# Weight splits of the state space part, given precedence over other work of ScalarE and VectorE

## The chip, the cores and the metric

The kernel runs on one core of one Trainium2 chip. The metric is the device time of one execution in microseconds (us). Of three runs of the kernel before, the median is 2339.6 us (2338.9 to 2342.73).

## The reference

Two networks run one after the other on 256 tokens of width 1024, all in float32. The first is one block of grouped-query attention, dilated window attention and a convolutional feed-forward. The second has two layers of a hybrid mixer over the 256 tokens and 256 context tokens: a differential attention beside a state space part (Mamba-2, both directions), merged by gates, and then a squared-ReLU MLP. Only the second network holds the changed part:

```python
xbc = dwconv_silu(xbc_raw, conv_w, conv_b)                # convolution of width 5, then SiLU
xs, bm, cm = jnp.split(xbc, [SSD_D_INNER, SSD_D_INNER + SSD_GROUPS * SSD_STATE], axis=-1)
# ssd_chunked, per direction, chunks of 128 tokens
cs = jnp.cumsum(dt * a, axis=chunk)
chunk_states = einsum(bc, exp(cs[-1] - cs), xc)
h[c + 1] = h[c] * exp(cs[-1]) + chunk_states[c]
y = einsum(cc @ bc.T, exp(cs[l] - cs[s]) below the diagonal, xc) + einsum(cc, h, exp(cs))
# ssd_output
return rmsnorm((yf + yb + d * xs) * jax.nn.silu(z), g) @ w_ssd_o
```

Here xbc_raw, z and the gates are products of the normalised tokens with slices of one wide weight matrix. There are 8 groups of 4 heads of 64, with a state of 128.

## The kernel before, in words

Activations lie transposed: 128 channels on the partitions, tokens along the free dimension. A float32 product is made of three float32r matmuls: weights and activations are both split in a high half, rounded to float32r, and a low half, the rest. `wload` (line 129) fetches 1 MB of weights (1024 rows, 256 columns) by a DMA on SP's queue into one of three `raw` buffers, and `wsplit` (line 138) makes of it two 128-column pieces, each with a copy to `whi` on ScalarE (line 145) and a subtraction to `wlo` on VectorE (line 146). Pool `whl` has four buffers of each half (line 820), that is two loads. A piece is then used by 24 matmuls (line 356), which take `hhi*whi`, `hlo*whi` and `hhi*wlo` in turn for eight steps of 128 rows.

`ssd` (line 1427) runs the state space part of a layer, with 512 tokens in layer 0 and 256 in layer 1 (the context's states are needed there too). It goes through 8 groups. For each group `front_g` makes B, C and x (tiles psB, psC, psxs, and after the convolution `conv` on VectorE the tiles BT, CT and xT) one group ahead, `z_g` makes the gate z (psz), and `fill_g` puts in products of other parts by a plan: in layer 0, groups 0 to 3 carry an attention output block with its gate (psga, psao), groups 4 to 6 carry none, group 7 a gate (psgs); in layer 1 most groups carry one block. In group 7, `so_g` begins the output product (psso).

The group's own work stands between these products. B and x are turned (ptB, ptx); `wx` scales x (tile xw, line 1553, VectorE) and `state` multiplies it with B into psst; `advance` makes the next state (hst, lines 1569 to 1572). `decay` builds the decay matrices E (lines 1590 to 1598) and R (1600, 1602) on ScalarE and VectorE from a row that a DMA on SP's queue spreads (`R<-csd`); `output` multiplies them with x and the states into psy. `decay` for the third and fourth chunk is traced right after the first and second `output`.

The order on TensorE is written out: with `self.pin` every matmul is kept in the order in which it is traced, and `Stream` feeds the products in steps between the group's own work. On ScalarE, VectorE and SP the framework's planner orders the queues when the program is built: among the instructions that it takes as ready at a moment it issues the one that was traced first. `high_priority(offset=n)` makes instructions count as if they had been traced n instructions earlier; the attention part uses it with 250 (`SOON`). On the chip each of these queues then runs in the planned order.

Of the kernel before, what the change touches and what calls it, by code (L numbers as in the profile page):

```python
# [12 lines left out]
F32 = mybir.dt.float32  # L13
# [12 lines left out]
ADD, SUB, MUL, MIN, MAX = ALU.add, ALU.subtract, ALU.mult, ALU.min, ALU.max  # L26
# [40 lines left out]

SOON = 250

CUTS = [slice(a, b) for a, b in ((0, 2), (2, 4), (4, 6), (6, 8))]  # L70

NWARM = 12
# [41 lines left out]
class Build:  # L114
    def __init__(self, tc, aps, es, stop=None):
        self.tc, self.nc, self.a, self.es, self.stop = tc, tc.nc, aps, es, stop
        self.pin = False

    def pool(self, name, bufs=1, space=None, reuse=None, side=None):
        kw = {} if side is None else {"side": side}  # L120
        if space is not None:
            kw["space"] = space
        if reuse:
            kw["reuse_waits"] = reuse
        return self.tc.tile_pool(name=name, bufs=bufs, **kw)
# [10 lines left out]
    def wsplit(self, raw, nk, cols):  # L136
        nc = self.nc
        w = []
        for c in range(0, cols, 128):
            n = min(128, cols - c)  # L140
            hi = self.whl.tile([P, 8, 128], F32R, tag="whi", name="whi")
            lo = self.whl.tile([P, 8, 128], F32R, tag="wlo", name="wlo")
            r = raw[:, :nk, c:c + n]
            h = hi[:, :nk, :n]
            nc.scalar.copy(h, r)  # L145
            nc.vector.tensor_tensor(out=lo[:, :nk, :n], in0=r, in1=h.bitcast(F32), op=SUB)  # L146
            w.append((hi, lo))
        return w

    def wloadB(self, src, pool, bufs):  # L150

        nc = self.nc
        raw = self.wraw.tile([P, 8, 256], F32, tag="raw", name="raw")
        nc.sync.dma_start(raw, src)
        hi = pool.tile([P, 8, 256], F32R, tag="whB", name="whB", bufs=bufs)
        lo = pool.tile([P, 8, 256], F32R, tag="wlB", name="wlB", bufs=bufs)
        for ks in (slice(0, 4), slice(4, 8)):
            self.split(hi[:, ks], lo[:, ks], raw[:, ks])
        return hi, lo
# [76 lines left out]
    def rsqrt(self, v, pool, n, tag="nw"):  # L236
        nc = self.nc
        p = v.shape[0]
        ti = pool.tile([p, n], F32, tag=tag + "t", name="nwt")
        y = pool.tile([p, n], F32, tag=tag + "y", name="nwy")  # L240
        nc.vector.tensor_scalar(out=ti.bitcast(I32), in0=v.bitcast(I32), scalar1=1, scalar2=None,
                                op0=ALU.arith_shift_right)
        nc.vector.tensor_scalar(out=y.bitcast(I32), in0=ti.bitcast(I32), scalar1=-1.0,
                                scalar2=float(0x5F3759DF), op0=MUL, op1=ADD)
        for _ in range(3):
            nc.vector.tensor_tensor(out=ti, in0=y, in1=y, op=MUL)
            nc.vector.scalar_tensor_tensor(out=ti, in0=ti, scalar=-0.5, in1=v, op0=MUL, op1=MUL)
            nc.vector.scalar_tensor_tensor(out=y, in0=ti, scalar=1.5, in1=y, op0=ADD, op1=MUL)
        return y

    def fnorm(self, src, kts, n, dim, pool):

        nc = self.nc
        acc = pool.tile([P, n], F32, tag="sqa", name="sqa")
        for i, k in enumerate(kts):
            if i == 0:
                nc.scalar.activation(out=acc, in_=src(k), func=AF.Square)
            else:
                sq = pool.tile([P, n], F32, tag="sq", name="sq", bufs=2)
                nc.scalar.activation(out=sq, in_=src(k), func=AF.Square)  # L260
                nc.vector.tensor_tensor(out=acc, in0=acc, in1=sq, op=ADD)
        return self.rstd([acc], n, dim, pool, root=False)
# [202 lines left out]
    def block1(self, xl, xc):  # L465
# [4 lines left out]
        with ExitStack() as es:  # L470
# [9 lines left out]
            wkv = [wf.tile([P, 8, 256], F32R, tag=n, name=n, bufs=2) for n in ("whB", "wlB")]  # L480
            for ks in CUTS:
                nc.sync.dma_start(xl[:, ks, :], a["x"][:, ks, :])
# [9 lines left out]
            with self.tc.manual_schedule(engines={ENG.DVE, ENG.Activation}):  # L492
                for ks in CUTS:
                    for k in range(ks.start, ks.stop):
# [932 lines left out]
    def ssd(self, l, hx, NQ, att):  # L1427
        nc, a = self.nc, self.a
        lat_only = NQ == 256
        tq = slice(0, NQ)  # L1430
        self.yd = None if lat_only else self.dr.tile([8, P, 512], F32, tag="yd", name="yd")
        ys = []
        SQ = self.ssq = self.cp.tile([P, 512], F32, tag="ssq", name="ssq")
        with ExitStack() as es:
            wk = es.enter_context(self.pool("ssd", reuse="tile"))
# [71 lines left out]
            for g in range(8):  # L1507
# [164 lines left out]
                for y, u in zip(yt, us):  # L1672
                    nc.vector.scalar_tensor_tensor(out=y, in0=y, scalar=0.5, in1=u, op0=MUL, op1=MUL)
                    if g == 0 and y is yt[0]:
                        nc.gpsimd.tensor_tensor(out=SQ, in0=y, in1=y, op=MUL)
                    else:
                        nc.scalar.activation(out=u, in_=y, func=AF.Square)
                        (nc.gpsimd if g < 7 else nc.vector).tensor_tensor(out=SQ, in0=SQ, in1=u, op=ADD)
                for j in range(2):
                    kt = 2 * g + j  # L1680
                    y = yy[j]
                    if self.yd is not None and kt < 8:
                        nc.sync.dma_start(self.yd[kt], y)
                        ys.append(None)
                    else:
                        if not lat_only or j == 0:
                            yhi = self.op.tile([P, 512], F32R, tag="op", name="yhi")
                            ylo = self.op.tile([P, 512], F32R, tag="op", name="ylo")
                        o = slice(j * 256, j * 256 + 256) if lat_only else slice(0, 512)
                        self.ysplit(l, kt, yhi[:, o], ylo[:, o], y)  # L1690
                        ys.append((yhi[:, o], ylo[:, o]))
        return ys

    def so_g(self, l, ys, NQ, c, i, ps=None):
# [448 lines left out]
```

## Time and profile before

| | us |
|---|---|
| median of 3 runs | 2339.6 |
| profiled execution | 2343.83 |
| its span, first to last instruction | 2342.0 |
| TensorE busy | 2297.6 |
| VectorE busy | 1821.4 |
| ScalarE busy | 1349.2 |

The granted TensorE clock is 0.998 of full speed over the span. The state space part of layer 0 lies at about 600 to 1066 us of the span, that of layer 1 at about 1757 to 2085 us. Busy times are of the engine, without its queue's waits. A matmul's end is modelled, so TensorE's busy share says little of how near it is to its peak; its idle time is what its queue waited for. In a list of waits a row reads: who waited, for whom, us in total, times, longest. In a timeline a row reads: start, duration, engine, line, operation, output and inputs, count, and in brackets the engine's idle time before it with what ended it.

### The profile page before, as it was taken

How to read it: one execution, taken by the hardware profiler on the slowest of the kernel's cores; microseconds unless marked ns; L12 is line 12 of the kernel's file. 1: busy time of each engine (PE TensorE's matmuls, PEld its weight loads, DVE VectorE, ACT ScalarE, POOL GpSimd, SP SyncE). 2: the span in 40 equal slices, each digit the busy share in tenths (PEclk: the TensorE clock that was granted, in tenths of full speed). 3: DMA queues.
4: the chain of work that ended last, by engine and by line, in shares of the span. 5: the costliest groups of instructions: out<-in, count | busy, mean ns of one | idle time of the engine just before them, and what ended most of it. 6: DMA issues, size and time to landing. Idle time of an engine off the chain costs nothing.

```text
span 2342.0 us, 38252 instructions
## 1 busy us (share of the span) xinstructions
PE 2297.6 (98%) x14840; PEld 2001.8 (85%) x14840; DVE 1821.4 (78%) x3601; ACT 1349.2 (58%) x2692; POOL 51.0 (2%) x61
## 2 busy tenths in 40 slices
PE   8999999999999999999999999999999999999998
PEld 8889989888887787778897878799898888899997
DVE  7678867877787788996476667488788999977887
ACT  5666546777666567774243223247776767655553
POOL 0000000000000000000000000000000000000000
PEclk9999999999999999999999999999999999999999
DMA  7557574212433334336235555362234535265553
GB/s 287 206 187 255 203 262 146 75 55 73 126 126 119 126 115 143 97 130 234 99 126 194 201 205 206 110 218 97 74 113 127 179 132 167 99 222 184 186 180 109
DMA packets 75894, 362.81 MB, mean 155 GB/s; under 512 B 9280, under 2 KB 16448, under 8 KB 38464
## 3 DMA queue, kind: packets, MB, share of 16 engines
q1 hardware_dynamic: 71952, 355.61, 44.4%
q10 hardware_dynamic: 3760, 4.75, 0.6%
q8 instruction: 117, 1.92, 0.3%
q14 instruction: 65, 0.53, 0.1%
HBM read 346.44 MB, written 13.89 MB: 154 GB/s over the span
## 4 chain that ended last, share of the span: by engine, by line
PE 73%; DVE 13%; ACT 9%; DMA 3%; issue 2%; SPq 0%; DVEq 0%; ACTq 0%
PE psm L356 20%; PE psxs L356 7%; PE psso L356 6%; PE psu L356 5%; PE psz L356 5%; PE psga L356 3%; PE pso L356 2%; PE psao L356 2%; PE psd L356 2%; PE psB L356 2%; PE psy L356 2%; DVE wlo L146 2%; PE psgs L356 2%; DMA araw<-in_ada 2%; PE psC L356 2%
## 5 line engine op out<-in xcount | busy, mean ns | idle before, releaser
L145 ACT CAST whi<-raw 128x1024 fp32r<-128x1024 f32 (+1 forms) x430 | 445.6, 1043 | 501.9 <-PE psm L356 234.2
L146 DVE TENSOR_TENSOR wlo<-raw,whi 128x1024 fp32r<-128x1024 f32 (+1 forms) x430 | 522.3, 1219 | 113.5 <-ACT whi L145 110.9
L356 PE MATMUL psm<-hhi,whi 128*128 128x258 f32 (+2 forms) x544 | 179.1, 329 | 1.7 <-ACT whi L145 1.2
L356 PE MATMUL psm<-hlo,whi 128*128 128x258 f32 (+2 forms) x544 | 178.5, 328 | 0.4 <-DVE hlo L1017 0.3
L356 PE MATMUL psm<-hhi,wlo 128*128 128x258 f32 (+2 forms) x544 | 178.1, 327 | 0.5 <-DVE wlo L146 0.5
L1590 ACT ACTIVATE E<-R,cstok 128x128 f32<-128x128 f32 x384 | 119.8, 391 | 37.8 <-PE psy L356 29.0
L356 PEld LDWEIGHTS psm<-hhi,whi 128*128 128x128 f32 x544 | 103.3, 190 | 16.0 <-ACT whi L145 4.3
L356 PE MATMUL psxs<-hhi,whi 128*128 128x512 f32 x256 | 112.6, 440 | 0.0
L356 PEld LDWEIGHTS psm<-hlo,whi 128*128 128x128 f32 x544 | 103.3, 190 | 10.6 <-DVE hlo L1017 1.2
L356 PE MATMUL psm<-dh,whi 128*128 128x512 f32 (+1 forms) x320 | 111.1, 347 | 0.5 <-DVE x L1902 0.5
L356 PEld LDWEIGHTS psm<-hhi,wlo 128*128 128x128 f32 x544 | 103.4, 190 | 9.4 <-DVE wlo L146 0.7
L356 PE MATMUL psm<-dl,whi 128*128 128x512 f32 (+1 forms) x320 | 111.1, 347 | 0.0
L356 PE MATMUL psm<-dh,wlo 128*128 128x512 f32 (+1 forms) x320 | 111.1, 347 | 0.0
L356 PE MATMUL psxs<-hhi,wlo 128*128 128x512 f32 x256 | 100.3, 392 | 0.0
L356 PE MATMUL psxs<-hlo,whi 128*128 128x512 f32 x256 | 100.2, 391 | 0.0
L1263 ACT ACTIVATE pr<-pss,mx 128x512 f32<-128x512 f32 (+1 forms) x96 | 58.4, 615 | 65.6 <-DVE mx L1261 65.3
L1450 DVE SCALAR_TENSOR_TENSOR xT<-psxs,halfw,xT 128x508 f32<-128x508 f32 (+1 forms) x128 | 94.9, 744 | 0.3
L356 PE MATMUL psu<-hhi,whi 128*128 128x256 f32 x320 | 91.4, 286 | 0.5 <-ACT hhi L897 0.5
L356 PE MATMUL psu<-hlo,whi 128*128 128x256 f32 x320 | 90.6, 283 | 0.8 <-DVE hlo L898 0.8
L356 PE MATMUL psz<-hhi,whi 128*128 128x512 f32 (+1 forms) x256 | 91.3, 356 | 0.0
L356 PE MATMUL psu<-hhi,wlo 128*128 128x256 f32 x320 | 90.5, 283 | 0.0
L356 PE MATMUL psm<-dhl,whi 128*128 128x512 f32 x256 | 89.5, 393 | 0.0
(500 smaller groups left out, 7105.6 us busy)
## 6 DMA issues: line engine op xcount, KB each, us to landing
raw<-in_w_m SPq DMA_DIRECT2D x68, 1024.0 KB, 4.9
araw<-in_ada SPq DMA_DIRECT2D x54, 1024.0 KB, 5.1
R<-csd SPq DMA_DIRECT2D x48, 512.0 KB, 6.0
raw<-in_w_up SPq DMA_DIRECT2D x22, 1024.0 KB, 5.0
raw<-in_w_qk SPq DMA_DIRECT2D x16, 1024.0 KB, 4.9
raw<-in_w_bc SPq DMA_DIRECT2D x16, 1024.0 KB, 5.2
raw<-in_w_xs SPq DMA_DIRECT2D x16, 1024.0 KB, 4.9
raw<-in_w_z SPq DMA_DIRECT2D x16, 1024.0 KB, 5.0
```

The lines of the kernel that those rows point to most:

```text
L145: nc.scalar.copy(h, r)
L146: nc.vector.tensor_tensor(out=lo[:, :nk, :n], in0=r, in1=h.bitcast(F32), op=SUB)
L356: i = self.nc.tensor.matmul(*args, **kw)
L1263: nc.scalar.activation(out=pt_[:, i * kw:(i + 1) * kw], in_=ps[:, i * kw:(i + 1) * kw], func=AF.Exp, scale=0.125, bias=mx[:, i:i + 1], acc ...
L1450: nc.vector.scalar_tensor_tensor(out=y[:, :, lo:hi], in0=u[:, :, lo + o:hi + o], scalar=wj(j), in1=y[:, :, lo:hi], op0=MUL, op1=ADD)
L1590: nc.scalar.activation(out=E[:, d, h, :], in_=R[:, d, h, :], func=AF.Relu, scale=-1.0, bias=self.cs_tok[:, c, i:i + 1])
```

## The change

A constant 150 is added. While `ssd` runs, `wsplit` issues its copy and its subtraction under `high_priority` with that offset. The tiles are allocated and the DMA is issued outside of it. Outside of `ssd` the offset is zero and nothing is different.

```diff
+WSOON = 150
...
         self.pin = False
+
+        self.wsoon = 0
...
             r = raw[:, :nk, c:c + n]
             h = hi[:, :nk, :n]
-            nc.scalar.copy(h, r)
-            nc.vector.tensor_tensor(out=lo[:, :nk, :n], in0=r, in1=h.bitcast(F32), op=SUB)
+            with self.tc.high_priority(offset=self.wsoon) if self.wsoon else ExitStack():
+                nc.scalar.copy(h, r)
+                nc.vector.tensor_tensor(out=lo[:, :nk, :n], in0=r, in1=h.bitcast(F32), op=SUB)
             w.append((hi, lo))
...
         ys = []
+        self.wsoon = WSOON
         SQ = self.ssq = self.cp.tile([P, 512], F32, tag="ssq", name="ssq")
...
                         ys.append((yhi[:, o], ylo[:, o]))
+        self.wsoon = 0
         return ys
```

## Rows read from the trace of the kernel before

**Rows 1.** The page, busy time: us, share of the span, instructions.

```profile
PE 2297.6 (98%) x14840; PEld 2001.8 (85%) x14840; DVE 1821.4 (78%) x3601; ACT 1349.2 (58%) x2692; POOL 51.0 (2%) x61
```

**Rows 2.** Busy time by stretch: stretch, length, busy us (instructions) by engine, clock, DMA.

```profile
690.00:886.00 196.00, 196.00 (x1040) 157.41 (x1040) 155.08 (x267) 121.46 (x260) 8.59 (x6) 1.00 0.41 130
918.00:1051.00 133.00, 129.91 (x740) 100.10 (x740) 127.93 (x237) 102.16 (x235) 9.46 (x6) 1.00 0.36 116
1783.00:1821.00 38.00, 36.19 (x205) 30.52 (x206) 36.58 (x63) 25.08 (x44) 0.00 (x0) 1.00 0.25 84
1821.00:2054.00 233.00, 232.90 (x1612) 203.66 (x1610) 220.14 (x357) 164.57 (x324) 8.89 (x6) 1.00 0.44 146
```

**Rows 3.** Waits of TensorE in the state space part of layer 0.

```profile
PE psst L356 <- DVE hst L1572: 1.5, 3, 0.8
PE psz L356 <- DVE wlo L146: 1.5, 2, 0.9
PE psy L356 <- DVE E L1598: 1.3, 2, 1.1
...
PE psB L356 <- DVE wlo L146: 0.2, 1, 0.2
```

**Rows 4.** Waits of TensorE in the state space part of layer 1.

```profile
PE psz L356 <- DVE wlo L146: 1.3, 1, 1.3
...
PE ptx L351 <- DVE xT L1454: 0.5, 1, 0.5
```

**Rows 5.** Timeline, layer 0, group 6: the second half of z.

```profile
993.60 1.05 ACT L145 CAST whi<-raw 128x1024 fp32r<-128x1024 f32 x1
...
1014.65 1.21 DVE L146 TENSOR_TENSOR wlo<-raw,whi 128x1024 fp32r<-128x1024 f32 x1
...
1015.92 0.50 PE L356 MATMUL psz<-hhi,wlo 128*128 128x512 f32 x1 [0.91 <-DVE wlo L146]
```

**Rows 6.** VectorE's groups of instructions, 918 to 1051: count, busy us, mean ns.

```profile
L146 DVE TENSOR_TENSOR wlo<-raw,whi 128x1024 fp32r<-128x1024 f32 x18 | 22.6, 1258 | 0.0
```

**Rows 7.** Timeline, layer 0, end of group 6: VectorE and TensorE.

```profile
1010.51 0.44 PE L356 MATMUL psy<-E,xd 128*64 128x128 f32 x4
...
1021.96 0.68 DVE L1598 TENSOR_TENSOR E<-E 128x512 f32<-128x512 f32 x1
...
1022.82 1.21 DVE L146 TENSOR_TENSOR wlo<-raw,whi 128x1024 fp32r<-128x1024 f32 x1
...
1022.82 0.44 PE L356 MATMUL psy<-E,xd 128*64 128x128 f32 x4
...
1024.28 0.50 PE L356 MATMUL psz<-hhi,whi 128*128 128x512 f32 x1
```

**Rows 8.** Timeline, layer 1: groups 0 and 2, around the first xw and psst.

```profile
1803.65 1.29 DVE L1553 TENSOR_TENSOR xw<-xd,dk 128x512 f32<-128x512 f32 x2
...
1805.47 1.02 PE L356 MATMUL psst<-xw,Bt 128*128 128x512 f32 x2
...
1878.15 1.04 ACT L145 CAST whi<-raw 128x1024 fp32r<-128x1024 f32 x1
...
1879.92 0.69 DVE L1553 TENSOR_TENSOR xw<-xd,dk 128x512 f32<-128x512 f32 x1
...
1880.03 1.04 ACT L145 CAST whi<-raw 128x1024 fp32r<-128x1024 f32 x1
...
1882.66 0.59 PE L356 MATMUL psst<-xw,Bt 128*128 128x512 f32 x1
...
1885.85 1.22 DVE L146 TENSOR_TENSOR wlo<-raw,whi 128x1024 fp32r<-128x1024 f32 x1
```

**Rows 9.** Waits of ScalarE and VectorE, 690 to 886, groups 1 to 3 of layer 0.

```profile
ACT whi L145 <- PE psz L356: 21.4, 6, 4.0
...
DVE wlo L146 <- ACT whi L145: 10.8, 10, 3.5
```

## The prediction

> **What bounds the kernel now.** I read the page first, then busy time by stretch, then who waits for whom on TensorE in the two state space parts, and last the order of single instructions around those waits.
>
> The page shows TensorE (PE) busy 98% of the span and VectorE (DVE) 78% [rows 1]. A busy PE need not be at its peak, but no order on other engines shortens a matmul; what this change can win lies in PE's idle time inside the state space parts. By stretch [rows 2] there are two regimes. In the plain groups PE never rests: 196.00 of 196 us in groups 1 to 3 of layer 0 and 232.90 of 233 in groups 1 to 6 of layer 1. In groups 4 to 7 of layer 0, which carry less filler for PE, and in the first group of layer 1, DVE is nearly full (127.93 of 133, 36.58 of 38) and PE is short: 133 - 129.91 = 3.1 and 38 - 36.19 = 1.8 us. PE's idle time in the four stretches is 0 + 3.1 + 1.8 + 0.1 = 5.0 us. The waits name the causes: in layer 0 psz and psB wait 1.5 + 0.2 us for a low half (wlo), psst 1.5 for hst, psy 1.3 for E [rows 3]; in layer 1 psz waits 1.3 for wlo, ptx 0.5 for xT [rows 4].
>
> **The change, part by part.** No instruction is added or removed, and the load's DMA on SP's queue keeps its place in the trace; only the 128-wide copies on ScalarE (ACT) and subtractions on DVE may go forward in their queues. They go past what was traced up to 150 instructions before them. In the full stretch of layer 0, 740 + 237 + 235 + 6 instructions take 133 us, 9.2 a us; in layer 1, 1612 + 357 + 324 + 6 take 233 us, 9.9 a us [rows 2]. So 150 stand for some 15 to 16 us (an estimate: it takes the planner's count as the profile's).
>
> *What goes.* The late low halves are late by their place in DVE's queue, not by their data: the second half of z in group 6 has its high half from 993.60, and DVE takes up the low half only at 1014.65; PE idles 0.91 us for it [rows 5]. With 15 us of precedence this one starts well before its use. All waits for low halves go: 1.5 + 0.2 + 1.3 = 3.0 us.
>
> *What is late next.* A low half takes 22.6 / 18 = 1.26 us in the full stretch [rows 6]. DVE has 133 - 127.93 = 5.1 us of idle time there [rows 2], so 1.26 us put in front of something is 1.26 us taken from it unless a gap takes it up. The next in line is E for the last psy of a group: it ends at 1021.96 + 0.68 = 1022.64, psy starts at 1022.82, and the low half for the next block begins only then [rows 7]. This E is traced after the psy two before its own, at 1010.51; the next load, group 7's z, is traced at its use, 1024.28 [rows 7]. The 13.8 us between them are less than 16, so both its halves can go ahead of E: 2 x 1.26 - 0.18 = 2.3 us of new wait. The bounds are 0 (the gaps of 5.1 us swallow it) and 2.3; I take 2.3, since that row shows DVE in step with PE and no gap before E. It is paid once and not in each group: in a stretch where DVE sets the pace, PE's total delay is fixed by the worst single point, and later waits shrink by what the earlier one took.
>
> In the first group of layer 1 the first xw ends about half way through the pair that begins at 1803.65 and takes 1.29, near 1804.3; psst uses it at 1805.47 [rows 8], a margin of about 1.1. Two low halves of 1.22 ahead of it cost 2.4 - 1.1 = 1.3 us. Bounds: 0 (they find a gap) and 1.3; I take 1.3, because this stretch has 38 - 36.58 = 1.4 us of DVE idle in all.
>
> In the plain groups of layer 1 (six in the stretch) the first xw ends at 1879.92 + 0.69 = 1880.6 and psst starts at 1882.66: 2.0 us of margin. The first high half of z starts at 1878.15 and is done at 1879.2, ahead of xw; the second starts at 1880.03, behind it [rows 8]. One low half ahead costs 1.22 < 2.0, so nothing; two would cost 0.4 in each of six groups, 2.6 us. I take 0 and keep 2.6 for the range. In groups 1 to 3 of layer 0 DVE has 196 - 155.08 = 41 us of idle time [rows 2] as cover, and most splits cannot move anyway (third rival): 0.
>
> *ACT and the buffers.* There are four buffers of each half, so a copy can start only when PE has done with the half four back. A copy that is first in ACT's queue holds everything behind it meanwhile: in groups 1 to 3 of layer 0 ACT stood 21.4 us in 6 such waits for psz, at most 4.0 us each, and DVE then 10.8 us in 10 waits for the copy [rows 9]. Earlier copies lengthen these waits. I take 0, since ACT has 233 - 164.57 = 68 us and DVE 13 us to spare in the plain groups of layer 1; without that cover it is the second rival. The Trainium skill says the same of the engines (TensorE: Matmul & The Clock Gate, "Architectural detail: the array is 16x 32x32, not 1x 128x128"): ScalarE and VectorE work their queues strictly first in, first out. The trace agrees with it in those 4.0 us, and it speaks against putting a waiting instruction forward.
>
> The Trainium skill's Perfetto Trace Analysis, "Optimization Strategy", advises to take the gaps of the bounding engine and to make what ends them start sooner. By that alone only the 3.0 us count and the time would be 2339.6 - 3.0 = 2336.6; here the engine that ends the gaps is itself full, which the 1.26 us above stand for.
>
> **Sum.** -3.0 + 2.3 + 1.3 + 0 = +0.6 us. The profiled execution took 2343.8 (span 2342.0 and 1.8 around it), which gives 2344.4; the runs' median of 2339.6 lies 4.2 lower, and I forecast by it: 2339.6 + 0.6 = 2340.2 us. What this kernel's measurement can tell from no change is about 0.2%, 4.7 us.
>
> **Rivals.**
> 1. *Faster: DVE's gaps take the early halves.* If the 5.1 us of DVE idle in layer 0 absorb what moves forward, and the raw buffers, free sooner, let loads start sooner, all of PE's 5.0 us may go: 2334.6. For it: the low halves are the largest single cause of waits. Against: the other 2.0 us have other causes (hst, E, xT), which early splits delay. Chance of more than 0.2%: 0.13.
> 2. *Slower: the queues stand at the split.* Place: z's and the fillers' copies in the six plain groups of layer 1. DVE idles 233 - 220.14 = 12.9 us there, 2.1 a group; from the point where the new standing exceeds 2.1 us a group, PE waits for all above. One standing of 4.0 us [rows 9] in every group costs 1.9 x 6 = 11 us; with the +0.6 and the 2.6 of xw that is 2354, and in half of the groups 2347. For it: 94% DVE, four buffers. Against: ACT has much slack, and copies already stand first there. Chance of more than 0.2%: 0.24.
> 3. *It changes little.* Where a copy already starts as its buffer comes free and the low half follows at once, as in the waits of [rows 9], precedence has nothing to overtake; only the full stretches change order, and a full DVE gives back what it gets. Time 2339.6. This shares the 0.63 of "within 0.2%" with my forecast.
>
> **How the numbers follow.** Likeliest is the forecast with the third rival: 0.63 within 0.2% (about 0.40 and 0.23). Faster 0.13, slower 0.24, as the first and second rival. The lower end is the first rival rounded, 2334: more than PE's 5.0 us can hardly go. The upper end is the second in somewhat over half the groups, 2349. Its own range for the likeliest case is 2336.6 (the 3.0 us go and nothing comes) to 2343 (+0.6 and 2.6).
>
> **What would show it right or wrong.** Right: PE's waits for wlo gone in both parts; low halves begin within a few us of their high halves in groups 5 to 7 of layer 0; there the waits of psst and psy for hst, xw and E grow by 1 to 3 us; the plain groups keep PE without idle time, as now. Wrong on the fast side: PE idle in layer 0's full stretch under 1.5 us with E still in time. Wrong on the slow side: PE waits of 1 us and more in the plain groups of layer 1, with longer waits of ACT for psz or psxs ahead of them; or DVE's idle time there above 13 us. If the low halves of group 6 still lag 20 us, the precedence does not reach as far as I take it to.

## The result: 18 us slower, and the profile after

The changed kernel took 2359.05 us in the median of 6 runs (2354.27 to 2363.47), the kernel before beside it 2340.96 in 6 runs (2338.9 to 2342.73): a ratio of 1.0079, 95% interval 1.0068 to 1.0089, or 18.1 us. The forecast was +0.6 us. The profiled execution took 2360.97 us, with a span of 2359.2 us against 2342.0, 17.2 us more. Matched matmul by matmul with the trace of before, it is 0.9 us late where layer 0's state space part begins and 6.8 where that ends, 5.4 where layer 1's begins and 17.2 where that ends: 5.9 us are lost in the one part and 11.8 in the other.

The work is the same. The page's first part has the same instructions, and VectorE's busy time, 1820.4 us, is that of [rows 1] within 2 us:

```profile
PE 2304.6 (98%) x14840; PEld 2008.0 (85%) x14840; DVE 1820.4 (77%) x3601; ACT 1351.1 (57%) x2692; POOL 50.4 (2%) x61
```

Busy time by stretch, the same four stretches of work as in [rows 2], moved by the delay so far. A row has the stretch, its length, the busy time of PE, PEld, DVE, ACT and POOL, the granted clock, and the DMA's share and rate:

```profile
691.00:888.00 197.00, 196.96 (x1047) 158.00 (x1047) 155.70 (x267) 122.62 (x263) 8.69 (x6) 1.00 0.40 130
919.00:1058.00 139.00, 131.19 (x742) 102.17 (x740) 128.26 (x236) 101.61 (x234) 8.85 (x6) 0.98 0.36 113
1790.00:1828.00 38.00, 35.84 (x197) 30.09 (x197) 35.24 (x60) 22.95 (x42) 0.00 (x0) 0.96 0.32 103
1828.00:2073.00 245.00, 237.81 (x1626) 207.16 (x1624) 220.41 (x359) 167.38 (x326) 8.70 (x6) 0.99 0.43 139
```

Groups 1 to 3 of layer 0 still run without idle time. The three others do not: PE idles 139 - 131.19 = 7.8 us where it idled 3.1, 38 - 35.84 = 2.2 where it idled 1.8, and in the six plain groups of layer 1 245 - 237.81 = 7.2 where it idled 0.1. That is 12.2 us more. VectorE idles more too (245 - 220.41 = 24.6 us in the plain groups, 12.9 before): it does not have more to do, it does it in a worse order. The clock of these three stretches is below 1.00 as well.

What PE waits for, in layer 0 and then in layer 1; the columns are the engine, the operation and what ended its wait, then us in total, times and the longest. They answer to [rows 3] and [rows 4]:

```profile
PE psst L361 <- DVE xw L1559: 6.6, 2, 3.7
PE psy L361 <- DVE E L1604: 1.8, 3, 1.1
PE psst L361 <- DVE hst L1578: 0.8, 1, 0.8
```

```profile
PE psy L361 <- DVE hst L1578: 5.6, 3, 2.1
PE ptx L356 <- DVE xT L1460: 2.2, 1, 2.2
PE psst L361 <- DVE xw L1559: 1.5, 1, 1.5
```

No wait for a low half is left in the two parts: the change did what it says, and its 3.0 us went. In groups 4 to 7 of layer 0 a low half now starts 0.7 us after its high half is done in the median and 4.4 at most, where it was 12.0 and 22.9. In their place stand waits for the state chain (xw, hst) and for xT, each long and in one piece. The two of 6.6 us stood at 954.01 (2.92 us, group 5) and 1002.38 (3.71 us, group 6). VectorE's queue around the second, in order of time (start, duration, instruction):

```profile
992.87 0.68 DVE L1559 TENSOR_TENSOR xw<-xd,dk 128x512 f32<-128x512 f32 x1
...
994.12 1.21 DVE L151 TENSOR_TENSOR wlo<-raw,whi 128x1024 fp32r<-128x1024 f32 x1
...
997.06 1.22 DVE L151 TENSOR_TENSOR wlo<-raw,whi 128x1024 fp32r<-128x1024 f32 x1
998.20 0.74 DVE L1456 SCALAR_TENSOR_TENSOR CT<-psC,halfw,CT 128x508 f32<-128x508 f32 x1
...
1001.16 0.74 DVE L1456 SCALAR_TENSOR_TENSOR CT<-psC,halfw,CT 128x508 f32<-128x508 f32 x1
1001.82 0.75 DVE L1559 TENSOR_TENSOR xw<-xd,dk 128x256 f32<-128x256 f32 x2
```

Two low halves, four steps of C's convolution, four steps of hst and two of E now stand between the second and the third xw (the row of 1001.82 holds the third and the fourth), and PE stands from 998.67 to 1002.38 for that third xw. In the kernel before, one low half, one step of C and one of hst stood between the same two:

```profile
990.51 0.67 DVE L1553 TENSOR_TENSOR xw<-xd,dk 128x512 f32<-128x512 f32 x1
...
991.76 1.21 DVE L146 TENSOR_TENSOR wlo<-raw,whi 128x1024 fp32r<-128x1024 f32 x1
...
994.49 0.41 DVE L1553 TENSOR_TENSOR xw<-xd,dk 128x256 f32<-128x256 f32 x1
```

From one xw to the other it is 8.95 us where it was 3.98. Of these 5.0 us the added low half takes 1.1; the three added steps of C take 2.0, those of hst 1.0 and of E 0.9. So the precedence did not only put pieces of 1.2 us in front of a fixed order: the planner set the order anew, and xw came out behind the convolution. In layer 1 the same happens to hst. Of group 2, first VectorE and then PE:

```profile
1888.31 1.21 DVE L151 TENSOR_TENSOR wlo<-raw,whi 128x1024 fp32r<-128x1024 f32 x1
...
1893.08 1.21 DVE L151 TENSOR_TENSOR wlo<-raw,whi 128x1024 fp32r<-128x1024 f32 x1
...
1899.95 1.23 DVE L151 TENSOR_TENSOR wlo<-raw,whi 128x1024 fp32r<-128x1024 f32 x1
...
1903.27 1.21 DVE L151 TENSOR_TENSOR wlo<-raw,whi 128x1024 fp32r<-128x1024 f32 x1
...
1906.06 1.21 DVE L151 TENSOR_TENSOR wlo<-raw,whi 128x1024 fp32r<-128x1024 f32 x1
1907.19 0.68 DVE L1460 SCALAR_TENSOR_TENSOR xT<-cth,xT 128x512 f32<-128x512 f32 x1
1907.79 0.41 DVE L1578 TENSOR_TENSOR hst<-hst,psst 128x256 f32<-128x256 f32 x1
```

```profile
1908.26 0.44 PE L361 MATMUL psy<-R,hst 128*64 128x128 f32 x4 [2.06 <-DVE hst L1578]
```

Five low halves, and behind the last of them the hst that PE waits 2.06 us for. Low halves are not denser than before; more of them stand ahead of this hst. Before, three stood between the first xw of the group (1879.92, [rows 8]) and this step, at 1885.85, 1887.64 and 1892.08, and it came 14.6 us after that xw:

```profile
1892.08 1.23 DVE L146 TENSOR_TENSOR wlo<-raw,whi 128x1024 fp32r<-128x1024 f32 x1
...
1894.47 0.42 DVE L1572 TENSOR_TENSOR hst<-hst,psst 128x256 f32<-128x256 f32 x1
```

Now it comes 20.7 us after it (1887.05 to 1907.79). Of the 6.2 us more, the two added low halves take 2.3, added steps of x's convolution 2.6. Groups 4 and 6 have the like at 1988.95 (1.95 us) and 2065.74 (1.60), group 5 a wait for xw at 2011.77 (1.48).

There is a second cost. The granted clock, by stretches of a few us:

```profile
951.00:954.00 3.00, 0.09 (x1) 0.02 (x1) 3.00 (x7) 0.67 (x2) 0.00 (x0) 1.00 0.86 319
954.00:957.00 3.00, 2.99 (x14) 2.54 (x14) 3.00 (x8) 1.15 (x4) 0.00 (x0) 1.00 0.02 8
...
1001.00:1007.00 6.00, 4.62 (x11) 3.70 (x12) 5.85 (x15) 2.43 (x6) 0.00 (x0) 0.50 0.24 101
...
1803.00:1806.00 3.00, 0.84 (x8) 0.61 (x7) 2.48 (x4) 2.03 (x3) 0.00 (x0) 1.00 0.00 0
1806.00:1810.00 4.00, 4.00 (x15) 3.08 (x14) 3.76 (x7) 1.22 (x2) 0.00 (x0) 0.57 0.42 119
1906.00:1909.00 3.00, 0.94 (x14) 0.74 (x12) 2.80 (x5) 0.63 (x1) 0.00 (x0) 0.94 0.35 55
1909.00:1912.00 3.00, 3.00 (x20) 2.67 (x17) 0.45 (x1) 2.44 (x8) 0.00 (x0) 0.50 0.87 347
```

From 1000.7 for 6.8 us, from 1806.3, 1908.7 and 1990.6 for 3.4 us each, the clock was at its lower level (0.50, which is 1.2 of 2.4 GHz); each began during a stall of 1.95 us or more or within 1.7 us of its end. The stall of 2.92 us that ended at 954.01 was followed by none. The kernel before has no such stretch in these parts. (A fifth, from 464.8, lies ahead of all that was changed; this execution loses 1.6 us there.) PE was busy for 5.12 + 3 x 3.4 = 15.3 us of them, and at half the clock up to 15.3 / 2 = 7.7 us of that is lost. With the 12.2 us of idle time it makes 19.9, an upper bound for the 17.2 us by which the span grew.

One stall shows the price of a stretch. In layer 1's first group PE waits 2.16 or 2.17 us for xT in six profiles. In three of them (the changed kernel, act_only, chain_after) 3.4 us at the lower clock go with it, and from the matmul at 1783 to the one at 1821 they lose 1.7, 1.7 and 1.7 us against the kernel before; in the others (dve_only, l1_only, pool_after) there are none, and they lose 0.2 each. So 3.4 us at the lower clock cost some 1.5 us there, and the 17 us of such stretches in the two parts some 7.5, an estimate.

### The profile page after: what moved, and what is told of

It reads as the page before. It is cut to its first block, busy times and chain, and to the rows that moved or that the text cites. A ratio compares the mean times of both kernels' runs of the same rounds, so it can differ in the third digit from the quotient of the medians.

```text
span 2359.2 us, 38322 instructions
## 1 busy us (share of the span) xinstructions
PE 2304.6 (98%) x14840; PEld 2008.0 (85%) x14840; DVE 1820.4 (77%) x3601; ACT 1351.1 (57%) x2692; POOL 50.4 (2%) x61
## 4 chain that ended last, share of the span: by engine, by line
PE 73%; DVE 14%; ACT 8%; DMA 3%; issue 2%; SPq 0%; DVEq 0%; ACTq 0%
PE psm L361 18%; PE psxs L361 6%; PE psso L361 6%; PE psu L361 5%; PE psz L361 5%; PE psao L361 3%; PE psga L361 3%; DVE wlo L151 3%; PE pso L361 2%; PE psd L361 2%; PE psy L361 2%; PE psB L361 2%; DMA araw<-in_ada 2%; PE psgs L361 2%; PE psC L361 2%
```

## Experiments

Each time is a median, beside runs of the kernel before on the same chip: 2340.87 us for the first four, 2341.55 for the next four, 2342.71 for the last four.

| run | us | ratio, 95% interval | us more |
|---|---|---|---|
| act_only | 2344.60 | 1.0016 [1.0007, 1.0025] | 3.7 |
| dve_only | 2361.14 | 1.0081 [1.0064, 1.0097] | 20.3 |
| l0_only | 2348.29 | 1.0032 [1.0020, 1.0044] | 7.4 |
| l1_only | 2348.42 | 1.0034 [1.0020, 1.0047] | 7.6 |
| chain_after | 2343.66 | 1.0013 [1.0003, 1.0022] | 2.1 |
| chain_before | 2347.81 | 1.0028 [1.0016, 1.0040] | 6.3 |
| off50 | 2343.62 | 1.0009 [0.9999, 1.0019] | 2.1 |
| z_only | 2347.03 | 1.0023 [1.0013, 1.0032] | 5.5 |
| pool_before | 2354.62 | 1.0050 [1.0037, 1.0063] | 11.9 |
| pool_after | 2356.87 | 1.0066 [1.0054, 1.0078] | 14.2 |
| l1_best | 2339.94 | 0.9989 [0.9980, 0.9997] | -2.8 |
| best | 2350.66 | 1.0041 [1.0029, 1.0053] | 8.0 |

**Which engine's queue.** The theory was VectorE's order; the rival, the prediction's second, that ScalarE's queue stands at copies whose buffer is not free. Each half of the change alone:

```diff
 # act_only: the copy alone has the precedence
+            with self.tc.high_priority(offset=self.wsoon) if self.wsoon else ExitStack():
+                nc.scalar.copy(h, r)
             nc.vector.tensor_tensor(out=lo[:, :nk, :n], in0=r, in1=h.bitcast(F32), op=SUB)
 # dve_only: the subtraction alone has it
             nc.scalar.copy(h, r)
+            with self.tc.high_priority(offset=self.wsoon) if self.wsoon else ExitStack():
+                nc.vector.tensor_tensor(out=lo[:, :nk, :n], in0=r, in1=h.bitcast(F32), op=SUB)
```

> Only the copies on ScalarE keep the precedence; the subtractions on VectorE go by their trace place again. Theory A (VectorE's order: low halves taken ahead of xw, hst and xT make TensorE wait): most of the loss goes, 2340 to 2346 us, TensorE's waits for xw and hst in the two state space parts under 3 us together. Theory B (ScalarE's queue stands at copies whose buffer is not free and holds back what VectorE needs): the loss stays, 2352 to 2360 us.

> Only the subtractions on VectorE keep the precedence. Theory A: the loss stays, 2352 to 2360 us, with waits of TensorE for xw and hst of 8 us and more. Theory B: 2339 to 2345 us, with ScalarE's waits for buffers as in the kernel before.

The subtraction alone costs all of it, 20.3 us, just above the range expected. The two stalls of psst in layer 0 are there, 3.10 and 3.70 us. PE's waits of dve_only in layer 1:

```profile
PE psst L361 <- DVE xw L1559: 5.5, 5, 1.5
PE ptx L356 <- DVE xT L1460: 2.2, 1, 2.2
PE psst L361 <- DVE hst L1578: 1.5, 2, 1.2
PE psy L361 <- DVE hst L1578: 1.1, 1, 1.1
```

In act_only, ScalarE does stand longer in the plain groups of layer 1, as the rival says (its waits there for psxs to free a buffer are 18.9 us, where before has 12.0), yet from the second group on PE's longest wait is 0.7 us; the xT of the first row is that of the first group:

```profile
ACT whi L150 <- PE psxs L361: 18.9, 8, 4.7
```

```profile
PE ptx L356 <- DVE xT L1460: 2.2, 1, 2.2
PE ptx L356 <- ACT xd L1550: 1.1, 2, 0.7
```

The rival is refuted as the main cause. One stall is its work all the same, that of xT in layer 1's first group. Of the changed kernel, ScalarE and then VectorE:

```profile
1803.20 1.04 ACT L150 CAST whi<-raw 128x1024 fp32r<-128x1024 f32 x1 [1.66 <-PE psC L361]
1804.15 0.62 ACT L1459 ACTIVATE cth<-xT 128x512 f32<-128x512 f32 x1
...
1804.81 0.69 DVE L1460 SCALAR_TENSOR_TENSOR xT<-cth,xT 128x512 f32<-128x512 f32 x1 [0.52 <-ACT cth L1459]
```

A copy stands 1.66 us for its buffer with the tanh of x's convolution (cth) behind it, and VectorE idles for that tanh before it makes the xT that PE waits 2.16 us for. In the kernel before this tanh ran at 1796.84, ahead of the copy at 1797.76. The same copy waits the same 1.66 us ahead of xT in act_only, dve_only and chain_after. The 3.7 us of act_only come with this late xT and 3.4 us at the lower clock behind it, and with waits for E and hst in layer 0 of 1.1 us at most.

**Which layer.**

```diff
 # l0_only
+        self.wsoon = 0 if lat_only else WSOON
 # l1_only
+        self.wsoon = WSOON if lat_only else 0
```

> Precedence in layer 0 alone. By the trace of the change, where layer 0's part came out 5.5 us later: 2346 us (2343 to 2349), with the two waits of psst for xw, 2.9 and 3.7 us, as in the full change, and nothing different in layer 1. If the two layers act on each other, it differs by more than 3 us.

> Precedence in layer 1 alone. By the trace of the change, 11 to 12 us later there, of which some 4 us stretches at half the clock: 2352 us (2347 to 2355). If the clock falls less often, near 2348.

By the medians the layers share the loss about equally (intervals of 4.7 to 10.3 and 4.7 to 11.0 us), and each shows the stalls that it has in the full change: 2.91 and 3.70 us for xw in l0_only, 2.16 for xT, 1.83, 1.94 and 1.60 for hst and 1.48 for xw in l1_only. The sum, 15.0 us, is 3.1 short of 18.1, which lies within the two intervals. The runs of l1_only differ with the clock: at a mean of 0.999 they took 2346.78 and 2346.99 us, at 0.998 2348.42 and 2348.55, and the profiled one at 0.996 2354.18. Not all of these 7 us is the layer's: of the profile's five stretches at the lower level two, of 3.4 us each, lie in its part. The one run of the full change at 0.998 took 2354.27, 13.3 us above the median of before.

**Is it the state chain?** If the loss comes from xw and hst behind low halves, putting these ahead again must take most of it away; put ahead without the change, they show what they cost by themselves.

```diff
 # chain_after: on the changed kernel; chain_before: the same on the kernel before
+                    with self.tc.high_priority(offset=300):
                         (the product xw)
+                        with self.tc.high_priority(offset=300):
                             (the two steps of hst in `advance`)
```

> The full change, and xw and the two steps of hst (VectorE) get precedence over the splits (offset 300). Theory A (the loss is the place of xw and hst behind low halves in VectorE's queue): TensorE's waits for xw and hst go from 14 us to under 3, the clock falls less, 2339 to 2345 us. Rival C (VectorE is simply full, and what is put first only decides what is late next): 2350 us and more, with new waits for E, xT or the convolution's tiles.

> The kernel before with the same precedence for xw and hst alone. Theory A: the waits of psst for hst and xw, 1.5 us in layer 0, go and little else changes: 2338 to 2341 us. Rival C: those of E and of the low halves grow by as much, 2341 to 2345 us.

chain_after gives back 16 of the 18 us. In layer 1 of its profile the waits of psy for hst and of psst for xw are gone, and of the group's own work only the xT of the first group is late, beside 0.3 us of psst for hst; in layer 0 the waits for xw are gone, and E, the next in line, is late instead:

```profile
PE psy L361 <- DVE E L1606: 6.6, 4, 3.0
...
PE ptx L356 <- DVE xT L1460: 2.2, 1, 2.2
```

chain_before is slower than either theory expected, and shows the other side of a full VectorE. There the state chain comes early and z's low half is late, once by 7.87 us, with 10.2 us at the lower clock. Its wait, then the instruction:

```profile
PE psz L356 <- DVE wlo L146: 9.0, 2, 7.9
```

```profile
1014.92 0.80 PE L356 MATMUL psz<-hhi,wlo 128*128 128x512 f32 x1 [7.87 <-DVE wlo L146]
```

**A smaller dose.**

```diff
 # off50
+WSOON = 50
 # z_only: WSOON = 150, set around z's loads in the groups alone
```

> The change with an offset of 50, about 5 us of the trace. Theory A: a split passes only what was traced less than a third as far back, so xw and hst, traced 2 to 4 us before their use, are still passed but by fewer splits: 2341 to 2348 us. If the loss does not depend on how far the splits come forward, 2355 us and more.

> Precedence for the loads of z alone, the only ones besides one of psB for which TensorE waited in the kernel before. Theory A: psz's waits (2.8 us) go, xw and hst still stand behind z's low halves in layer 1's groups and in groups 5 and 6 of layer 0: 2344 to 2354 us. If precedence hurts through other loads (x, B, C), 2338 to 2342 us.

A third of the reach costs 2.1 us, an interval that holds no change: PE waits 4.2 us for hst and 3.8 for E in layer 0, none longer than 1.7, and the clock stays up in both parts. z's loads alone bring back one stall of 4.0 us in layer 0, a stretch of 6.8 us at the lower clock that begins in it, and 5.5 us. Neither wins anything in all.

**Is VectorE's load or its order the limit in layer 0?** GpSimd is nearly idle there, so z's low halves of groups 4 to 7 went to it.

```diff
 # pool_before: on the kernel before; pool_after: on the changed one
+            (nc.gpsimd if self.lo_pool else nc.vector).tensor_tensor(out=lo[:, :nk, :n], ...
+                self.lo_pool = l == 0 and g > 3     # around z's loads
```

> The kernel before, with one edit: the low halves of z's weight in groups 4 to 7 of layer 0 (8 of them) are subtracted by GpSimd, which is idle there, instead of VectorE. Theory A (VectorE is full in that stretch, so whatever stands last in its queue makes TensorE wait, and order alone cannot win): 8 x 1.26 = 10 us leave VectorE, its idle time there rises from 5 to some 15 us, TensorE's waits in layer 0 fall from 5.2 to under 3 us, 2337 to 2340. Rival (the order of VectorE's queue alone makes the waits, its load does not): TensorE's waits stay at 4 to 5 us, 2341 within 1. Should GpSimd's subtraction take so long, or slow VectorE's own work so much, that the halves come late, TensorE waits for the low half for several us a group: 2345 and more.

> The full change, with the low halves of z's weight in groups 4 to 7 of layer 0 on GpSimd. Theory A: the two single stalls of psst in layer 0 (2.9 and 3.7 us) shrink to under 1 us each and the slow-clock stretch behind the second goes, while layer 1 keeps its own loss of some 7 us: 2347 to 2351. Rival (the stalls come from order, of which load takes no part, for example from the fillers' low halves ahead of xw): the two stalls stay above 2 us, 2355 to 2360.

Both miss the range of their theory. The expectation of pool_before allowed for a slowed VectorE, but through low halves that come late, and none is late. GpSimd's subtractions and, below them, what VectorE did in the same moments in pool_before:

```profile
996.53 2.38 POOL L147 TENSOR_TENSOR wlo<-raw,whi 128x1024 fp32r<-128x1024 f32 x1 [5.47 <-ACT whi L146]
1005.94 2.40 POOL L147 TENSOR_TENSOR wlo<-raw,whi 128x1024 fp32r<-128x1024 f32 x1 [7.03 <-ACT whi L146]
1011.01 2.37 POOL L147 TENSOR_TENSOR wlo<-raw,whi 128x1024 fp32r<-128x1024 f32 x1 [2.67 <-ACT whi L146]
```

```profile
996.83 2.62 DVE L1556 TENSOR_TENSOR xw<-xd,dk 128x512 f32<-128x512 f32 x1
...
1006.17 2.45 DVE L1649 TENSOR_TENSOR hst<-hst,dec 128x256 f32<-128x256 f32 x1
...
1009.87 0.41 DVE L1574 TENSOR_TENSOR hst<-hst,dec 128x256 f32<-128x256 f32 x1
...
1011.13 2.92 DVE L1600 SCALAR_TENSOR_TENSOR E<-cb,dttok,E 128x128 f32<-128x128 f32 x3
```

An xw of 0.68 us takes 2.62, a step of hst of 0.41 takes 2.45, and each ends 0.3 to 0.7 us after GpSimd's instruction does. What reads PSUM was not held: the BT step on psB at 947.11, beside the subtraction from 946.50 to 949.43, took its 0.73 us. Nor was an xw that began with that subtraction, at 946.51 (0.68 us). All six subtractions between 918 and 1062 us show it; the excess of the six VectorE entries that they hit is 1.94 + 2.04 + 2.05 + 1.5 + 2.0 + 1.6 = 11.1 us (the groups of E against three times 0.29 and against 1.13). What left VectorE is 6 x 1.26 = 7.6. So by these entries the move loads VectorE by 3.5 us where it is fullest, in lumps of 2 us (over the whole stretch, 921 to 1064.3, it is busy 133.1 us where it was 127.9), and 11.9 us are lost. In pool_after the stalls of 2.9 and 3.7 us for xw are gone and the longest waits of psst are 1.84 and 1.83 us, for hst; but psy waits 1.82 for E, and layer 1 has its own loss; the time is the rival's, the shorter stalls are the theory's. Whether load is the limit in layer 0 can't be told from this, since the load did not fall.

**A better order for layer 1.** There VectorE has some 2 us to spare in each group. l1_best leaves layer 0 as it was and orders layer 1 by what PE needs first; best adds the GpSimd edit of layer 0.

```diff
 # l1_best; best = l1_best with the edit of pool_before
+        self.wsoon = WSOON if lat_only else 0
+                    with self.tc.high_priority(offset=400) if lat_only and g == 0 else ExitStack():
                         conv(ps, 512, 2 * g + j, t)          # the x part
+                    with self.tc.high_priority(offset=300) if lat_only else ExitStack():
                         (xw, and in `advance` the two steps of hst)
```

> The change in layer 1 alone, with the state chain put ahead of it: the splits there have the precedence of 150, xw and the two steps of hst 300, and the convolution of the x part in layer 1's first group 400. Layer 0 is as before. Theory A (layer 1's VectorE has some 2 us of slack a group, so an order that serves the state chain first and the splits next has no waits): the stalls of psy for hst (2 us in three groups) and of ptx for xT (2.2) go, and the 1.3 us of psz in the first group as well: 2338.5 to 2340.5 against 2341. Rival (what is put back then is late in its turn, as in layer 0): a new stall of over 1 us in layer 1 and 2342 to 2346.

> Both of these: layer 1 with the state chain ahead of the splits, and z's low halves of groups 4 to 7 of layer 0 on GpSimd. Theory A: the two gains add up, TensorE idles under 3 us in the two parts together, 2335.5 to 2339. Rival (either edit gives nothing): 2340 to 2346.

l1_best is the fastest kernel of the study: 2339.94 us in 11 runs against 2342.71 in 17, 0.9989 with an interval of 0.9980 to 0.9997. Its first group of layer 1 and the plain groups:

```profile
1783.00:1821.00 38.00, 37.75 (x228) 32.23 (x228) 35.95 (x60) 26.41 (x50) 0.00 (x0) 1.00 0.35 114
...
1821.00:2054.00 233.00, 232.94 (x1610) 203.71 (x1610) 221.42 (x362) 166.14 (x323) 8.83 (x6) 1.00 0.44 147
```

PE's idle time in the first group is 0.25 us where it was 1.8, with the plain groups as full as before: the 1.3 us for the low half are won here and nothing takes their place. That is 1.6 of the 2.8 us; the rest is within the interval, which puts the gain at 0.7 to 4.7 us. The three edits were not tried apart, but z_only and off50, which move splits alone, also pass this group 1.5 us sooner than the kernel before, so its gain is the splits'. best misses its range: it loses as pool_before does, and at 8.0 us stands 3.9 below it.

## Why the prediction was wrong

*That waits for low halves go, 3.0 us:* right, in both layers.

*"It is paid once and not in each group":* wrong, and the place too. E for the last psy of group 6, priced at 2.3 us, costs 0.30 (the psy at 1028.86), and all waits for E 1.8 us, where [rows 3] has 1.3. The wait that came was xw's, in group 5 (2.92 us) and again in group 6 (3.71). The step failed because it took the order of all else as fixed and asked only which instruction the next low half would overtake. The planner re-sorted the queue: all four steps of the convolution of C went ahead of the third xw, where one had, and of the 5.0 us by which that xw came later only 1.1 are a low half. The net forecast for this stretch, 2.3 - 1.5 - 0.2 = 0.6 us, came out as 4.7 us of idle time and 6.8 us at the lower clock; l0_only puts the layer at 7.4 us.

*First group of layer 1, 1.3 us:* the net of idle time was near (2.2 us against 1.8; forecast no change), but by luck: the wait is for xT and not for xw, and it comes through ScalarE's queue, which *ACT and the buffers* put at 0 for the spare time of ScalarE and VectorE. Spare time did not help: the copy stood 1.66 us at the head of the queue and the tanh with it. With the lower clock behind it the group lost 1.7 us.

*"I take 0" for the plain groups of layer 1:* the step that failed most. It weighed one low half of 1.22 us against the 2.0 us of xw's margin, and did not price hst, the next link of the same chain. Nor did it price what else came ahead with the low halves: in group 2 five low halves instead of three stand between the first xw and the second hst, and four more steps of x's convolution, and this hst follows its xw 6.2 us later than before. PE's idle time in these groups rose by 7.1 us, and l1_only measures 7.6 for the layer.

*Not counted at all:* that one wait of 2 us may cost more than 2 us, through the clock. The sum of waits was the whole price in the prediction.

*The second rival* had a place (plain groups of layer 1) and the sign; its 2347 to 2354 falls short of 2359. It did not have the cause there: ScalarE's standing grew, to 24.1 us for psxs in the full change, and act_only shows it to be nearly free in these groups. Its mechanism came in the first group, at the one xT. The rule cited there from the Trainium skill (TensorE: Matmul & The Clock Gate, "Architectural detail: the array is 16x 32x32, not 1x 128x128"), that both engines work their queues in strict order, was held against ScalarE's queue alone; the trace agrees with it on VectorE, where xw and hst stood behind low halves (3.71 and 2.06 us of PE's time). The *third rival* failed since the splits did find things to overtake. The prediction's own marks for the slow side came true, PE waits of 1 us and more in the plain groups and VectorE's idle time there above 13 us (24.6); the longer waits of ScalarE that it puts ahead of those waits are there and are not the cause.

What stays open: how the 18.1 us divide between idle time and the lower clock (no run tried it apart; some 7.5 us of clock is an estimate from one stall, for one execution), and whether any order wins in layer 0, where xw, E and the low halves each were late in one run.

## What to carry to other kernels

When an engine that is nearly full is told to do one kind of work sooner, price every consumer of that engine's queue within the reach of the move, and count all that comes to stand ahead of it, not the moved work alone; the planner may re-sort the rest as well. Work that only has to be ready by its use (a split of weights) goes behind the chain that returns to the bounding engine (xw, psst, hst, psy): with the chain put first in layer 1, the splits cost nothing there and l1_best won 2.8 us (0.7 to 4.7). In these runs short stalls were cheaper than a long one: off50 has waits of 8 us in layer 0, none over 1.7 and none with the lower clock behind it, and loses 2.1 us, where z_only's single 4.0 us goes with 6.8 us at the lower clock and a loss of 5.5.

## What the runs showed of the hardware

- In the two parts of all profiles, 16 of the 23 stalls of TensorE of 2.0 us and more had a stretch at the lower clock begin in them or within 2 us of their end, of 3.4 to 10.2 us, and 5 of the 14 of 1.5 to 2.0 us. The length of a stall alone does not decide it: of the changed kernel's, one of 1.95 us was followed and one of 2.92 us was not; the same stall in dve_only (3.10 us, ended at 954.84) was, from 955.8.
- GpSimd's 128x1024 subtraction took 2.37 to 3.12 us, where VectorE's takes 1.22, and in each of six cases held a VectorE instruction that began beside it until it was over (0.41 became 2.45 us). The Trainium skill has this (Trainium Architecture — The Big Picture, "What this means for kernel authors"): the two engines share a pair of ports, under an exclusive lock. The rows above agree.
